# Expert loop of a two-layer MoE trunk: queues held in program order, weights split two pieces ahead

## The chip, the cores and the metric

One core of a Trainium2 chip runs the whole program. Its engines work side by side, each from its own queue: TensorE (matmuls; PE, its weight loads PEld), VectorE (DVE), ScalarE (ACT), GpSimd (POOL) and SyncE (SP, which here only issues loads). The metric is the time of one execution on the device, in microseconds. An instruction waits at the head of its engine's queue until what it needs is there.

## The reference

A trunk of two residual layers on 512 tokens of width 1024, all in fp32. Layer 0 mixes tokens with a state-space and a pooling mixer, layer 1 with stick-breaking attention. Behind each mixer stands the feed-forward part that the change touches:

```
x   = LN(alpha*x + mixer(x))
ple = (p[i] @ Wp) * sigmoid(x @ Wg)
s   = sigmoid(x @ Wr);  best group of 4 experts, then its top 2 of 16 by s + bias;  gates = s normed
h   = silu(x @ w1[e]) * (x @ w3[e])        # 1024 -> 512, for each expert e
ffn = sum_e gates[e] * (h @ w2[e])         # 512 -> 1024
x   = LN(alpha*x + ffn + ple)
```

Each expert has 6 MB of weights (w1, w3, w2), so a layer loads 96 MB of them.

## The kernel before

Each layer's feed-forward part is `ffn`. It sorts the experts by their number of tokens and visits them in a fixed mix, `SEQ`, of ten "big" ones (96 rows of tokens each) and six "small" ones (64 rows). A token's two rows are gathered from DRAM by GpSimd (`gather`), transposed by TensorE into `g` (`load_g`), and an expert's results are scattered back (`scatter`). Rows beyond 96 or 64 go through `overflow`, code in a branch at expert 12 that is skipped when a flag is 0, as here.

A matmul of a big expert is made of three fp32r matmuls (`mm3`): the weights and the tokens are split into a high part (ScalarE's copy to fp32r, L89) and a low part (VectorE's subtraction, L90), and high*high, high*low, low*high are added. A small expert is multiplied in plain fp32 from the raw weights, with w1 and w3 side by side in the array.

Weights come in pieces of 1 MB: four for `up` (w1 and w3, two halves `kh` each) and two for `down`. `plan_ffn` writes the pieces into a list in the order of use: up(e+1, 0), down(e), up(e+1, 1), and so on, with the two pieces of a gate block after expert 7 and of the last one at the end (`GATES`). `prefetch` walks that list and issues loads on SP into "raw" slots (17 of 8 KB a partition, which also hold x, its transposes and `g`). `weights` takes the next piece, splits it on the spot into tiles of two rings (5 high and 6 low tiles; a piece takes two of each) and hands them to the matmuls. `plain` hands out the raw piece of a small expert.

The program is written as: act(e), up(e+1, 0) first piece, turn(e) (transposes of the activation), up(e+1, 0) second piece, down(e), output copies `ysb` (L1147), scatter, load_g(e+2), up(e+1, 1). PSUM has four banks A (up), two B (down and the gate block in the loop), two T (transposes).

The order in which the instructions stand in an engine's queue is not the written one: a scheduler places them, by priority (written order) and by a cost model's idea of when each becomes ready, and it may put a later instruction ahead. The split of a piece is written directly ahead of the matmuls that use it.

Of the kernel before, what the change touches and what calls it, by code (L numbers as in the profile page):

```python
# [2 lines left out]

# [8 lines left out]
AF = mybir.ActivationFunctionType  # L12
# [13 lines left out]
NH = 5  # L26
GATES = (-1, -1, 7, 15)
OVER = 12
SMALL = 64
BIG = 10  # L30
SEQ = (1, 2, 11, 3, 4, 12, 5, 6, 13, 7, 14, 8, 15, 9, 16, 10)
# [10 lines left out]
class Trunk:  # L42
    def __init__(self, ctx, tc, I, out, dbg=None, stop=99):
        self.tc, self.nc, self.I, self.out = tc, tc.nc, I, out
        self.dbgs = dbg or {}
        self.stop = stop
        self.cp = ctx.enter_context(tc.tile_pool(name="cp", bufs=1))
        self.sb = ctx.enter_context(tc.tile_pool(name="sb", bufs=1))
        self.ps = ctx.enter_context(tc.tile_pool(name="ps", bufs=1, space=bass.MemoryType.PSUM))
        self.dp = ctx.enter_context(tc.tile_pool(name="dp", bufs=1, space=bass.MemoryType.DRAM))  # L50
        self.queue = []
        self.loaded = 0
        self.used = 0
        self.raws = {}
        self.cat = None
        self.limit = None
        self.ends = {}
        self.order = {}
        self.eid = {}
# [58 lines left out]
            self.raws[self.loaded] = t  # L118
            self.loaded += 1

    def weights(self, ahead, pool=False):
        i = self.used
        self.prefetch(i + 1 + ahead)
        self.used += 1
        _, k, n, _ = self.queue[i]
        raw = self.raws.pop(i)
        kh = min(k, 1024 // n)
        out = []
        for a in range(0, k, kh):
            h, l = self.ring_pair(f"w{i}_{a}")  # L130
            self.split(h[:, :kh * n], l[:, :kh * n], raw[:, a * n:(a + kh) * n], pool)
            h, l = (t[:, :kh * n].rearrange("p (k n) -> p k n", k=kh) for t in (h, l))
            out += [(h[:, q, :], l[:, q, :]) for q in range(kh)]
        return out

    def consts(self):
        nc, cp = self.nc, self.cp
# [819 lines left out]
    def ffn(self, layer, last):  # L957
# [40 lines left out]
        def gate(c):  # L998
            for _ in gate_parts(c):
                pass  # L1000

        ng = GATES.count(-1)
        pr = self.bank("B", "pB")
# [10 lines left out]
        def rows(e):  # L1014
            return SMALL if SEQ[e] > BIG else CAP

# [19 lines left out]
        def load_g(e):  # L1036
            c = rows(e)
            if c == CAP:
                self.gtile = self.slot(f"g{layer}_{e}", F32R)
                g = self.gtile[:, :2 * KB * c].rearrange("p (a k t) -> p a k t", a=2, k=KB)  # L1040
            else:
                g = self.slot(f"g{layer}_{e}")[:, :KB * c].rearrange("p (k t) -> p k t", k=KB)
            for hf in range(2):
                p = self.bank("T", "pT")[:, :4 * c]
                for k in range(4):
                    nc.tensor.transpose(p[:, k * c:(k + 1) * c], xgs[:c, e % 2, hf * 512 + k:(hf + 1) * 512:4],  # L1046
                                        self.ident[:c, :c])
                ks = slice(hf * 4, hf * 4 + 4)
                p = p.rearrange("p (k t) -> p k t", k=4)
                if c == CAP:  # L1050
                    self.split(g[:, 0, ks], g[:, 1, ks], p)
                elif hf:
                    v.tensor_copy(g[:, ks], p)
                else:
                    nc.scalar.activation(g[:, ks], p, AF.Copy)
            if e + 2 < NE:
                gather(e + 2)
            return e, g

        def banks(e):  # L1060
            return [self.bank("A", "pA") for _ in range(2 if rows(e) == CAP else 1)]

        def up(eg, hh, kh, a):
            e, g = eg
            if rows(e) == CAP:
                w = self.weights(LA)
                for k in range(4):
                    kb = kh * 4 + k
                    self.mm3(hh[a][:CAP], (g[:, 0, kb], g[:, 1, kb]), w[k], kb == 0, kb == KB - 1)
                return  # L1070
            if a == 0:
                self.pair = [self.plain(LA), self.plain(LA)]
            for k in (2 * a, 2 * a + 1):
                kb = kh * 4 + k
                for x in range(2):
                    nc.tensor.matmul(hh[0][x * 64:x * 64 + 64], g[:, kb], self.pair[x][:, k], start=(kb == 0),  # L1076
                                     stop=(kb == KB - 1))

        def act(e, hh):
            t = self.half4("sg")  # L1080
            if rows(e) == CAP:
                sg = t[:CAP, :512]
                nc.scalar.activation(sg, hh[0][:CAP], AF.Silu)
                v.tensor_tensor(sg, sg, hh[1][:CAP], op=OP.mult)  # L1084
                return sg
            nc.scalar.activation(t[64:128, :512], hh[0][0:64], AF.Silu)
            sg = t[0:64, 512:]
            v.tensor_tensor(sg, t[64:128, :512], hh[0][64:128], op=OP.mult)
            return sg
# [16 lines left out]
        def down(e, sT):  # L1106
            hs = [slice(nh * 512, (nh + 1) * 512) for nh in range(2)]
            if rows(e) == CAP:
                py = [self.bank("B", "pB")[:CAP] for _ in hs]
                for a in range(2):  # L1110
                    w = self.weights(LA)
                    for q in range(2):
                        k = 2 * a + q
                        for x, h in enumerate(hs):
                            self.mm3(py[x], (sT[:, 0, k], sT[:, 1, k]), [t[:, h] for t in w[q]], k == 0, k == 3)
            else:
                p = self.bank("B", "pB")
                py = [p[x * 64:x * 64 + 64] for x in range(2)]
                for a in range(2):
                    w = self.plain(LA)  # L1120
                    for q in range(2):
                        k = 2 * a + q
                        for x, h in enumerate(hs):
                            nc.tensor.matmul(py[x], sT[:, k], w[:, q, h], start=(k == 0), stop=(k == 3))  # L1124
            yield from zip(hs, py)

        self.limit = self.ends[layer]
# [3 lines left out]
        for _ in early:  # L1131
            pass
        hh = banks(0)
        up(g, hh, 0, 0)
        up(g, hh, 0, 1)
        gn = load_g(1)
        up(g, hh, 1, 0)
        up(g, hh, 1, 1)
        for e in range(NE - 1):
            sg = act(e, hh)  # L1140
            hh = banks(e + 1)
            up(gn, hh, 0, 0)
            sT = turn(e, sg)
            up(gn, hh, 0, 1)
            ysb = self.half4("ysb")
            for h, py in down(e, sT):
                nc.scalar.activation(ysb[:rows(e), h], py, AF.Copy)  # L1147
            scatter(e, ysb)
            if e == OVER:
                self.overflow(layer, xd, yd)  # L1150
            if e in GATES:
                gate(GATES.index(e))
            g = gn
            if e + 2 < NE:
                gn = load_g(e + 2)
            if e == NE - 3:
                oht = self.last_onehot(self.gtile[:, 2 * KB * CAP:])
                self.ln_setup("ln_ffn", layer)
            up(g, hh, 1, 0)
            up(g, hh, 1, 1)  # L1160
        yts = []
        for i in range(NT):
            yt = self.slot(f"yt{layer}_{i}")
# [161 lines left out]
    def plan_ffn(self, layer):  # L1325
        I = self.I
        wg = I["ple_w_gate"][layer]
        wp = I["ple_w_proj"][layer]

        def gate(c):  # L1330
            self.plan(wg[:, c * 256:(c + 1) * 256], 8, 256)
            self.plan(wp[:, c * 256:(c + 1) * 256], 2, 256)

        def part(e, n, rs, cs=slice(None)):
            r = SEQ[e]
            if r <= 2:
                return I[n][layer, r - 1, rs, cs]

            def dyn():
                x = self.expert(layer, r)  # L1340
                return None if x is None else I[n][layer, bass.ds(x, 1), rs, cs]
            return dyn

        def up(e, kh):
            for n in ("moe_w1", "moe_w3"):
                self.plan(part(e, n, slice(kh * 512, (kh + 1) * 512)), 4, 512, True)

        for c in range(GATES.count(-1)):
            gate(c)
        up(0, 0)  # L1350
        up(0, 1)
        for e in range(NE):
            if e + 1 < NE:
                up(e + 1, 0)
            for nh in range(2):
                self.plan(part(e, "moe_w2", slice(nh * 256, (nh + 1) * 256)), 2, 1024, True)
            if e in GATES:
                gate(GATES.index(e))
            if e + 1 < NE:
                up(e + 1, 1)  # L1360
        self.ends[layer] = len(self.queue)
# [61 lines left out]
```

## Time and profile before

| | |
|---|---|
| three runs | 1269.9, 1266.07, 1269.86 us (median 1269.86) |
| the profiled execution | 1270.47 us, span of its trace 1268.7 us |
| TensorE busy | 1155.3 us, 91% of the span |
| VectorE, ScalarE, GpSimd busy | 790.2, 595.3, 129.7 us |
| mean granted TensorE clock | 0.953 of 2.4 GHz |
| DMA | 285.05 MB, mean 225 GB/s |
| expert loop of layer 0 | about 236 to 552 us of the span |
| expert loop of layer 1 | about 913 to 1225 us of the span |

Matmuls overlap in the pipeline, so the time of a group of them is read from start to start. A row of the waits says which engine and line waited for which, the sum, the number of waits and the longest. The granted clock is a share of 2.4 GHz; at any moment it is 1.0 or 0.5.

### The profile page before, as it was taken

To read this page: it belongs to the slowest core of one execution; us is meant where nothing else is said; L and a number is where in the kernel's file an instruction comes from. 1 tells how busy PE (TensorE), PEld (TensorE's weight loads), DVE (VectorE), ACT (ScalarE), POOL (GpSimd) and SP (SyncE) were. 2 spreads that over 40 slices of the span, in tenths; PEclk is the share of its full clock that TensorE was granted. 3 is DMA by queue.
4 is the path that set the end of the run, shared out by engine and by line. 5 is a ranking of instruction groups with operands and counts; after the bars stand their busy time and mean duration, and the time that the engine had idled before them with its cause. 6 is when DMAs were issued, how large, how long until landed. Compare 5 with 4: busy or idle time off the path is not lost. (4 is left out here: it accounts for less than half of the span.)

```text
span 1268.7 us, 16688 instructions
## 1 busy us (share of the span) xinstructions
PE 1155.3 (91%) x6191; PEld 819.9 (65%) x6191; DVE 790.2 (62%) x1249; ACT 595.3 (47%) x895; POOL 129.7 (10%) x153
## 2 busy tenths in 40 slices
PE   6958989999899887899999999998999899987895
PEld 5847779756467544576867767688865467544564
DVE  7997775765475443477477467756777465453465
ACT  4313531756464443453365456523466455444451
POOL 5010020111010110001000000010111110110001
PEclk9988999999899997799999999998999899988898
DMA  8226651699897996873112014434399997997941
GB/s 254 59 79 210 261 174 65 230 366 395 344 335 287 360 367 234 324 256 100 34 42 92 1 67 159 159 133 142 107 385 373 370 347 267 377 340 279 365 181 66
DMA packets 83663, 285.05 MB, mean 225 GB/s; under 512 B 18816, under 2 KB 42896, under 8 KB 57936
## 3 DMA queue, kind: packets, MB, share of 16 engines
q1 hardware_dynamic: 70032, 256.56, 54.2%
q0 software_dynamic: 8800, 25.19, 6.1%
q10 hardware_dynamic: 4736, 2.10, 0.6%
q8 instruction: 52, 0.85, 0.3%
q14 instruction: 43, 0.35, 0.1%
HBM read 270.45 MB, written 18.61 MB: 228 GB/s over the span
## 5 line engine op out<-in xcount | busy, mean ns | idle before, releaser
L90 DVE TENSOR_TENSOR w_0l<-raw,w_0h 128x1024 fp32r<-128x1024 f32 (+1 forms) x161 | 192.2, 1194 | 59.2 <-ACT w_0h L89 58.4
L89 ACT ACTIVATE w_0h<-raw 128x1024 fp32r<-128x1024 f32 (+1 forms) x161 | 166.4, 1033 | 49.7 <-PE pG L96 27.2
L90 DVE TENSOR_TENSOR w_2l<-raw,w_2h 128x1024 fp32r<-128x1024 f32 x93 | 113.4, 1220 | 47.7 <-ACT w_2h L89 47.6
L89 ACT ACTIVATE w_2h<-raw 128x1024 fp32r<-128x1024 f32 x93 | 97.9, 1053 | 48.2 <-PE pA L96 40.7
L94 PE MATMUL pA<-w_0h,g 128*96 128x512 f32 x160 | 71.5, 447 | 35.4 <-ACT g L89 35.4
L1076 PE MATMUL pA<-raw,g 128*64 128x512 f32 x384 | 97.3, 620 | 0.0
L1147 ACT ACTIVATE ysb<-pB 96x512 f32<-96x512 f32 (+1 forms) x60 | 35.3, 591 | 105.2 <-PE pB L1124 58.8
L1019 POOL DMA_INDIRECT xg<-xd,ixm x32 | 34.4, 1076 | 409.2 <-PE pT L1046 339.2
L95 PE MATMUL pA<-w_0l,g 128*96 128x512 f32 x160 | 67.7, 423 | 3.2 <-DVE w_0l L90 3.2
L96 PE MATMUL pA<-w_0h,g 128*96 128x512 f32 x160 | 68.3, 427 | 2.0 <-DVE g L90 1.9
L94 PEld LDWEIGHTS pA<-w_0h,g 128*96 128x96 f32 x160 | 28.3, 177 | 59.1 <-ACT g L89 44.3
L94 PE MATMUL pA<-w_2h,g 128*96 128x512 f32 x160 | 65.9, 412 | 0.0
L96 PE MATMUL pA<-w_2h,g 128*96 128x512 f32 x160 | 65.3, 408 | 0.0
L95 PE MATMUL pA<-w_2l,g 128*96 128x512 f32 x160 | 65.3, 408 | 0.0
L1026 POOL DMA_INDIRECT yd<-ysb,ixm x30 | 35.3, 1175 | 228.2 <-ACT ysb L1147 180.1
L1076 PEld LDWEIGHTS pA<-raw,g 128*64 128x64 f32 x384 | 25.8, 139 | 43.5 <-issue 39.9
L90 DVE TENSOR_TENSOR w_1l<-raw,w_1h 128x1024 fp32r<-128x1024 f32 x40 | 48.8, 1219 | 3.6 <-ACT w_1h L89 3.2
L696 DVE TENSOR_TENSOR_SCAN kw<-kw 128x128 f32<-128x128 f32 (+3 forms) x64 | 50.3, 813 | 0.9 <-ACT kw L693 0.6
L1046 PEld LDWEIGHTS pT<-ident,xg 96*128 96x128 f32 (+1 forms) x256 | 34.8, 215 | 22.5 <-issue 15.0
L89 ACT ACTIVATE w_1h<-raw 128x1024 fp32r<-128x1024 f32 x40 | 42.0, 1051 | 10.6 <-PE pA L96 10.6
L1046 PE MATMUL pT<-ident,xg 96*128 96x96 f32 (+1 forms) x256 | 37.0, 285 | 10.7 <-PEq L1231 5.0
L1084 DVE TENSOR_TENSOR sg<-sg,pA 96x512 f32<-96x512 f32 x20 | 13.6, 682 | 48.6 <-PE pA L96 48.6
(469 smaller groups left out, 2909.6 us busy)
## 6 DMA issues: line engine op xcount, KB each, us to landing
raw<-in_moe_w_dram SPq DMA_DIRECT2D x192, 1024.0 KB, 8.3
raw<-in_sb_w_qkv_dram SPq DMA_DIRECT2D x12, 1024.0 KB, 6.0
raw<-in_ple_w_gate_dram SPq DMA_DIRECT2D x8, 1024.0 KB, 8.6
yt<-yd SPq DMA_DIRECT2D x8, 1024.0 KB, 7.9
raw<-in_ab_w_out_dram SPq DMA_DIRECT2D x4, 1024.0 KB, 6.5
xd<-x0r POOLq DMA_DIRECT2D x8, 512.0 KB, 4.0
raw<-in_sb_w_out_dram SPq DMA_DIRECT2D x4, 1024.0 KB, 5.8
raw<-in_ab_w_in_dram SPq DMA_DIRECT2D x3, 1024.0 KB, 8.8
```

The costliest lines, as they stand in the source:

```text
L89: return (self.nc.scalar.activation(hi, src, AF.Copy), (self.nc.gpsimd if pool else self.nc.vector).tensor_tensor(lo, src, hi.bitcast(F32) ...
L90: (self.nc.gpsimd if pool else self.nc.vector).tensor_tensor(lo, src, hi.bitcast(F32), op=OP.subtract))
L94: t.matmul(out, s[0], m[0], start=first, stop=False)
L95: t.matmul(out, s[0], m[1], start=False, stop=False)
L96: t.matmul(out, s[1], m[0], start=False, stop=last)
L696: v.tensor_tensor_scan(rv, rv, rv, 1.0, op0=OP.mult, op1=OP.min)
L1019: return nc.gpsimd.indirect_dma_start(out=xgs[:c, e % 2, :], out_offset=None, in_=xd[:, :], in_offset=bass.IndirectOffsetOnAxis(ap=self.ix ...
L1026: nc.gpsimd.indirect_dma_start(out=yd[:, :], out_offset=bass.IndirectOffsetOnAxis(ap=self.iy[:c, r:r + 1], axis=0), in_=src[:c], in_offset ...
L1046: nc.tensor.transpose(p[:, k * c:(k + 1) * c], xgs[:c, e % 2, hf * 512 + k:(hf + 1) * 512:4], self.ident[:c, :c])
L1076: nc.tensor.matmul(hh[0][x * 64:x * 64 + 64], g[:, kb], self.pair[x][:, k], start=(kb == 0), stop=(kb == KB - 1))
L1084: v.tensor_tensor(sg, sg, hh[1][:CAP], op=OP.mult)
L1147: nc.scalar.activation(ysb[:rows(e), h], py, AF.Copy)
```

## The change

Two things. `weights` is cut in two: `cut` splits a piece, `weights` takes a piece that was split earlier if there is one. A new `ahead` splits on from the next piece, skipping pieces of small experts (`whole`), until two split pieces stand ready or four pieces have been looked at; it is called after each piece that TensorE uses in the expert loop and after the gate block. And the body of the loop, now `step` and `rest`, runs under `ordered`, which ties every instruction of TensorE, ScalarE and VectorE to the one written before it on the same engine, so that the scheduler keeps the written order in these three queues. SP and GpSimd are not tied, nor is the code outside the loop.

```diff
+ENGINES = (mybir.EngineType.PE, mybir.EngineType.Activation, mybir.EngineType.DVE)
...
+        self.ready, self.whole, self.chain, self.chained = {}, set(), {}, None
...
-    def weights(self, ahead, pool=False):
-        i = self.used
-        self.prefetch(i + 1 + ahead)
-        self.used += 1
-        _, k, n, _ = self.queue[i]
-        raw = self.raws.pop(i)
+    def cut(self, i):
+        raw, (_, k, n, _) = self.raws.pop(i), self.queue[i]
...
+    def weights(self, ahead):
+        i = self.used
+        self.prefetch(i + 1 + ahead)
+        self.used += 1
+        return self.ready.pop(i) if i in self.ready else self.cut(i)
+
+    def ahead(self, depth):
+        i = self.used
+        self.prefetch(i + depth)
+        while len(self.ready) < 2 and i < min(self.loaded, self.used + 4):
+            if i not in self.ready and i not in self.whole:
+                self.ready[i] = self.cut(i)
+            i += 1
+
+    @contextmanager
+    def ordered(self):
+        block = self.nc.cur_bb
+        traced = block.bb.instructions
+        start = len(traced)
+        yield
+        assert self.nc.cur_bb is block
+        last = self.chain if self.chained is block else {}
+        for i in traced[start:]:
+            if i.engine in ENGINES:
+                if i.engine in last:
+                    self.tc.add_manual_dep(i, last[i.engine], mybir.DependencyInfo(
+                        mybir.DependencyClass.NoSync, mybir.DependencyReason.DATA), reason="order")
+                last[i.engine] = i.name
+        self.chain, self.chained = last, block
...
             for _ in gate_parts(c):
                 pass
+            self.ahead(LA)
...
+                self.ahead(LA)      # in up() and down(), after each piece's matmuls
...
+        def step(e, hh, gn):
+            with self.ordered():
+                sg = act(e, hh)
+                hh = banks(e + 1)
+                up(gn, hh, 0, 0)
+                sT = turn(e, sg)
+                up(gn, hh, 0, 1)
+                ysb = self.half4("ysb")
+                for h, py in down(e, sT):
+                    nc.scalar.activation(ysb[:rows(e), h], py, AF.Copy)
+            scatter(e, ysb)
+            return hh
+
+        def rest(e, hh, g):
+            gn = None
+            with self.ordered():
+                if e in GATES:
+                    gate(GATES.index(e))
+                if e + 2 < NE:
+                    gn = load_g(e + 2)
+                if e == NE - 3:
+                    self.oht = self.last_onehot(self.gtile[:, 2 * KB * CAP:])
+                up(g, hh, 1, 0)
+                up(g, hh, 1, 1)
+            if e == NE - 3:
+                self.ln_setup("ln_ffn", layer)
+            return gn
+
         for e in range(NE - 1):
-            sg = act(e, hh)
...
+            hh = step(e, hh, gn)
             if e == OVER:
                 self.overflow(layer, xd, yd)
-            if e in GATES:
-                gate(GATES.index(e))
...
+            gn = rest(e, hh, gn)
...
+            if r > BIG:
+                self.whole.add(len(self.queue))
```

The two up calls of expert 0 and `load_g(1)` between them, ahead of the loop, are put under `ordered` too.

## Rows read from the trace of the kernel before

**Rows 1.** Page, engines: busy us (share of the span) x instructions.
```profile
PE 1155.3 (91%) x6191; PEld 819.9 (65%) x6191; DVE 790.2 (62%) x1249; ACT 595.3 (47%) x895; POOL 129.7 (10%) x153
```

**Rows 2.** Windows: both loops and stretches; first line names the columns.
```profile
core 0: us, PE busy (x) PEld busy (x) DVE busy (x) ACT busy (x) POOL busy (x), PEclk, DMA share, GB/s
236.00:552.00 316.00, 288.03 (x1300) 175.75 (x1299) 169.60 (x187) 163.30 (x208) 32.91 (x30) 0.94 0.86 326
913.00:1225.00 312.00, 287.74 (x1302) 175.97 (x1301) 170.21 (x187) 163.31 (x209) 33.09 (x30) 0.94 0.88 330
236.00:391.00 155.00, 147.46 (x682) 93.37 (x681) 94.19 (x98) 90.70 (x114) 20.09 (x17) 0.98 0.95 361
...
327.00:340.00 13.00, 7.55 (x22) 3.84 (x17) 6.34 (x7) 7.75 (x10) 0.00 (x0) 0.74 0.93 363
...
495.00:507.00 12.00, 6.49 (x25) 2.83 (x25) 3.37 (x4) 3.31 (x5) 0.00 (x0) 0.72 0.58 205
518.00:538.00 20.00, 15.12 (x59) 11.32 (x56) 6.16 (x8) 8.13 (x11) 0.00 (x0) 0.66 0.85 320
```

**Rows 3.** Waits of TensorE, 236 to 552 us: total us, times, longest us.
```profile
PE pA L94 <- ACT g L89: 17.7, 6, 5.0
PE pT L1046 <- DVEq L1231: 2.9, 1, 2.9
PE pT L1046 <- PEq L1231: 2.7, 1, 2.7
PE pA L95 <- DVE w_0l L90: 1.6, 2, 0.9
```

**Rows 4.** Waits of TensorE, 913 to 1225 us; the other terms as in rows 3.
```profile
PE pT L1046 <- PEq L1231: 2.3, 1, 2.3
```

**Rows 5.** Timeline of TensorE: start us, us, instruction, count, [idle before <- releaser].
```profile
279.80 0.47 PE L94 MATMUL pA<-w_0h,g 128*96 128x512 f32 x1
...
282.76 3.65 PE L1124 MATMUL pB<-raw,sT 128*64 128x512 f32 x16
...
313.17 1.94 PE L1076 MATMUL pA<-raw,g 128*64 128x512 f32 x8
...
332.87 0.74 PE L94 MATMUL pA<-w_0h,g 128*96 128x512 f32 x1 [5.01 <-ACT g L89]
```

**Rows 6.** Timeline of ScalarE around that wait.
```profile
322.68 1.29 ACT L1147 ACTIVATE ysb<-pB 96x512 f32<-96x512 f32 x2 [3.55 <-PE pB L96]
327.94 0.59 ACT L1086 ACTIVATE sg<-pA 64x512 f32<-64x512 f32 x1 [3.96 <-PE pA L1076]
328.55 1.06 ACT L89 ACTIVATE w_0h<-raw 128x1024 fp32r<-128x1024 f32 x1
...
332.35 0.85 ACT L89 ACTIVATE g<-pT 128x384 fp32r<-128x384 f32 x2
```

**Rows 7.** Timeline of SP: issue of two weight loads.
```profile
302.44 0.33 SPq L117 DMA_DIRECT2D raw<-in_moe_w_dram  x1
...
424.82 0.33 SPq L117 DMA_DIRECT2D raw<-in_moe_w_dram  x1
```

**Rows 8.** DMA issues, 236 to 552 us: count, size, median us to landing.
```profile
raw<-in_moe_w_dram SPq DMA_DIRECT2D x86, 1024.0 KB, 8.4
```

**Rows 9.** Groups by form, 236 to 391 us: busy us, mean ns | idle before.
```profile
L89 ACT ACTIVATE w_0h<-raw 128x1024 fp32r<-128x1024 f32 x34 | 35.8, 1053 | 3.6 <-PE pA L96 2.6 <-PE pB L96 1.0
...
L90 DVE TENSOR_TENSOR w_0l<-raw,w_0h 128x1024 fp32r<-128x1024 f32 x34 | 41.4, 1219 | 8.9 <-ACT w_0h L89 8.7
...
L1084 DVE TENSOR_TENSOR sg<-sg,pA 96x512 f32<-96x512 f32 x6 | 4.1, 682 | 13.0 <-PE pA L96 13.0
```

**Rows 10.** Timeline of VectorE: the last expert's one-hot.
```profile
510.65 1.62 DVE L1218 TENSOR_SCALAR ohl<-slotrow,keep,sel 128x128 f32<-128x128 bf16 x6
```

**Rows 11.** Timeline of TensorE: the one-hot's matmuls.
```profile
524.96 3.75 PE L1219 MATMUL pT<-ident,ohl 128*128 128x128 f32 x16 [0.82 <-DVE g L90]
```

**Rows 12.** Waits of SP, 236 to 552 us: total us, times, longest us.
```profile
SPq L117 <- DVE w_2l L90: 91.2, 28, 11.8
```

**Rows 13.** Timeline of ScalarE: the copy of the piece issued at 424.82.
```profile
438.36 1.05 ACT L89 ACTIVATE w_0h<-raw 128x1024 fp32r<-128x1024 f32 x1
```

More of the change, by code (lines that the diff above doesn't have):

```diff
@@ L1 @@
 import math
-from contextlib import ExitStack
+from contextlib import ExitStack, contextmanager
 import concourse.bass as bass
@@ L130, in weights @@
             h, l = self.ring_pair(f"w{i}_{a}")
-            self.split(h[:, :kh * n], l[:, :kh * n], raw[:, a * n:(a + kh) * n], pool)
+            self.split(h[:, :kh * n], l[:, :kh * n], raw[:, a * n:(a + kh) * n])
             h, l = (t[:, :kh * n].rearrange("p (k n) -> p k n", k=kh) for t in (h, l))
@@ L1077, in up @@
                                      stop=(kb == KB - 1))
+            self.ahead(LA)
         def act(e, hh):
@@ L1115, in down @@
                             self.mm3(py[x], (sT[:, 0, k], sT[:, 1, k]), [t[:, h] for t in w[q]], k == 0, k == 3)
+                    self.ahead(LA)
             else:
@@ L1124, in down @@
                             nc.tensor.matmul(py[x], sT[:, k], w[:, q, h], start=(k == 0), stop=(k == 3))
+                    self.ahead(LA)
             yield from zip(hs, py)
@@ L1133, in ffn @@
         hh = banks(0)
[L1134 to L1138, printed above, removed]
-        for e in range(NE - 1):
-            sg = act(e, hh)
[L1141 to L1148, printed above, removed]
+        with self.ordered():
+            up(g, hh, 0, 0)
+            up(g, hh, 0, 1)
+            gn = load_g(1)
+            up(g, hh, 1, 0)
[14 more added lines that the diff above has]
+            gn = None
+            with self.ordered():
+                if e in GATES:
[4 more added lines that the diff above has]
+                    self.oht = self.last_onehot(self.gtile[:, 2 * KB * CAP:])
+                up(g, hh, 1, 0)
+                up(g, hh, 1, 1)
+            if e == NE - 3:
+                self.ln_setup("ln_ffn", layer)
+            return gn
+        for e in range(NE - 1):
+            hh = step(e, hh, gn)
             if e == OVER:
                 self.overflow(layer, xd, yd)
-            if e in GATES:
-                gate(GATES.index(e))
[L1153 to L1160, printed above, removed]
+            gn = rest(e, hh, gn)
+        oht = self.oht
         yts = []
```

## Prediction

> **What bounds the kernel now.** I read the page's engine shares first, then two stretches of the trace, then who waits for whom in them. TensorE is busy 91% of the span [rows 1]; nothing else is near that, so time is won only where TensorE stands still or runs at half clock. The change touches the two expert loops, 236 to 552 us and 913 to 1225 us. There TensorE is busy 288.0 of 316 us and 287.7 of 312 us, so it stands still 28.0 and 24.3 us, and the granted clock has a mean of 0.94 in both [rows 2]. The clock has two levels, 1.2 and 2.4 GHz, so a mean of 0.94 means that 12% of the stretch runs at half rate; 6% of its work time is lost: 0.06 x 316 = 19 us and 0.06 x 312 = 18.7 us. About 47 us of one loop and 43 us of the other are therefore not work. I call that the prize, 90 us in all.
>
> What makes the idle time? In the first loop 17.7 us lie in six waits for one thing, ScalarE's copy of the gathered tokens `g` (L89), before the first matmul of a 96-row ("big") expert; 1.6 us are two waits for VectorE's half of a weight split; 5.6 us are the branch around the overflow code (L1231) [rows 3]. The remaining 3.1 us I leave standing. The second loop repeats 17.7 and 1.6 to the digit and has 2.3 us at the branch [rows 4].
>
> The longest of these waits shows why. TensorE idles 5.01 us before 332.87 [rows 5]. ScalarE copied the last expert's output at 322.68, then did nothing for 3.96 us, because the next entry in its queue was the small expert's `sg`, which needs TensorE's last matmul. Only behind it stood four weight copies (328.55 on) and, behind those, the copy of `g` at 332.35 [rows 6]. So the queue held ready work behind an entry that was not ready. The data had long been there: the first of the two pieces (by its place in the plan) was issued at 302.44 [rows 7], and the median landing is 8.4 us after issue [rows 8], so it lay in SBUF from about 311, 17 us before its copy. It was a question of order, not of supply.
>
> The clock follows: over 327 to 340 us it is 0.74 granted, 13 x 0.26 = 3.4 us lost on top of the 5.01. At the branch (495 to 507) 0.72, 3.4 us; over 518 to 538, where a 4 us wait runs into the one-hot matmuls, 0.66, 6.8 us [rows 2]. Of the first loop's 19 us that leaves 8.8 for the stretches behind the other `g` waits.
>
> **The change, part by part.** (1) After each piece of weights the code now splits on until two pieces stand ready, past the whole (unsplit) pieces of small experts. Read off the program order: while TensorE does the down projection before a small expert's second half, ScalarE and VectorE now split the next big expert's first two pieces, and `g` of the expert after is copied right behind the output copy. Both are what TensorE waited for. So the 17.7 and the 1.6 go: 19.3 us in each loop. (2) Their half-clock stretches go with them: 8.8 us, and half of the 6.8 behind the one-hot (the half that the `g` wait began, 3.4): 12.2 us, taken alike for the second loop, whose mean clock is the same. Gross: 31.5 us a loop, 63 us in all.
>
> Now what comes instead. (3) Does the held order keep pace? A piece of a big expert costs TensorE 2.96 us (279.80 to 282.76, twelve matmuls) [rows 5]; ScalarE two copies of 1.05, 2.1 us, VectorE two subtractions of 1.22, 2.44 us [rows 9]. Over an expert VectorE needs 12 x 1.22 = 14.6 us and some 2.5 for `g`, `sg` and `sT`, 17.1 against TensorE's 6 x 2.96 and 1.9 of transposes, 19.7. It keeps pace with 2.6 us to spare. The ring has 5 high tiles, a piece takes two, so of the piece two ahead the second half can only be written when TensorE is halfway through the piece in use; TensorE then needs it no sooner than 4 us later.
>
> (4) The tight spot is a big expert followed by a small one (six a loop): TensorE covers the activation with 1.94 us only [rows 5]. The last ring pair is released 1.48 us before TensorE ends the expert; copy 1.05, subtraction 1.22, so VectorE is free 0.8 us after that end, does `sg` in 0.68 [rows 9], and the transposes can start at 1.5: 0.4 us to spare. If VectorE is one subtraction late it is 0.8 us short. That bounds it between 0 and 6 x 0.8 = 4.8 us a loop (less than nothing it cannot be, the waits of before being counted already). I take 2, nearer to the row-by-row working than to the late case.
>
> By the Trainium skill's PSUM — Partial Sum matmul accumulation buffer (Engine vs sequencer instructions) ScalarE and VectorE work their queues strictly first in, first out. That speaks against part (1) as much as for it: a split that has to wait, for a landing or for the ring, now holds up every activation behind it. Rows 6 agree, with 3.96 us of that very kind; the sum by it alone is that of the slower rival below.
>
> (5) The gate block inside the loop now follows expert 7's down projection directly, and both PSUM banks it could use hold that projection's output. The first of the two output copies takes half of 1.29 us [rows 6]; with the handoff 0.9 us of waiting. Bounds 0 (another bank order) and 1.3 (both copies).
>
> (6) The last expert's one-hot now stands in the held order, straight behind the copies of `g`, and ahead of a small expert's matmuls. VectorE made six of its eight comparisons in 1.62 us before, beside other TensorE work [rows 10]; now TensorE must wait for 8 x 0.27 = 2.2 us and for the two transpose banks. Its own 16 records took 3.75 us at half clock [rows 11] and are no new work. I take 3 us, between 0 (hidden as before) and 6 (nothing overlaps, clock low).
>
> (7) The overflow branch stays; its 5.6 and 2.3 us and its half clock are in neither sum.
>
> (8) Loads. The plan's order of loads and SP's queue are not touched, but SP's waits are mostly for VectorE's subtractions to free a raw slot (91.2 us in 28 waits for one tile group) [rows 12], so earlier splits issue loads earlier. The loop needs 0.86 x 316 = 272 us of DMA time; in its first half the share was already 0.95 [rows 2]. If the loop shrinks to 292 us, the share must be 0.93. That is near what has been seen, not over it. The tightest piece found: issued 424.82 [rows 7], landing some 8.4 later at 433.2, copied 438.36 [rows 13]: 5 us of margin where the new order wants it about 3 us sooner. I price it at 2 us a loop, between 0 and the rival's 17.
>
> Sum: 63 - 2 x (2 + 0.9 + 3 + 2) = 63 - 16 = 47 us. The profiled execution took 1270.5 us, its span is 1268.7; it is 0.6 above the median of the runs shown, 1269.9. So 1270.5 - 47 - 0.6, about 1223; I write 1222.
>
> **Rivals.** *Loads become the bound.* For it: small experts hold raw slots until TensorE has used them, and in the loop's second half small and big alternate. Against: the 17 us above. If the share reaches only 0.90, a loop lasts 272 / 0.90 = 302 us, 14 us gained each: 1270 - 28 = 1242.
>
> *Nothing new costs.* The one-hot and the gate hide and the steps stay tight: all 63 and up to 12 more from the clock at the one-hot and the branch: 1195 to 1207.
>
> *The held queue stalls TensorE (slower).* At each of the 15 steps of a loop the split two pieces ahead stands in ScalarE's and VectorE's queues before the activation, and waits for the ring or a landing. Place: the transposes of `sg` after the first piece of the next expert. From 63 / 30 = 2.1 us a step on the kernel loses; at 3 us, one copy, one subtraction and `sg` in a row (1.05 + 1.22 + 0.68), it is 90 - 63 = 27 slower: 1297. Against: VectorE's 2.6 us to spare per expert.
>
> *It does not do what it says.* Order and splits stay in effect what they were, since ring or raw slots give no room: 1268 to 1272. Against: when TensorE waited 5 us the ring was empty and the data 17 us old. By the Trainium skill's Perfetto Trace Analysis (Optimization Strategy) gaps that repeat can mean that there is no buffer for the next tile; by that rule a new order would win nothing. These gaps do repeat, but the trace has the cause in the order of ScalarE's queue.
>
> **How the numbers follow.** Forecast, 1207 to 1236: 0.57. Loads: 0.20. Nothing new costs: 0.10. Slower: 0.07. No effect: 0.06. The likeliest is 1222. The range takes the forecast's own, most of the loads' case and half of the cheap one: 1198 to 1250. A measurement of this kernel can tell about 0.3%, 4 us: faster 0.57 + 0.20 + 0.10 = 0.87, same 0.05, slower 0.08.
>
> **What would show it.** Right: in the waits of TensorE in the two loops the `ACT g L89` line falls from 17.7 us to under 3; the loops take 285 to 298 us; DMA share in them 0.90 or more; the half clock is left at the branch and the one-hot. (4) is wrong if waits of the transposes (L1096) for `sg` pass 5 us in a loop; (6) if the one-hot's waits pass 6; (8) if TensorE's or ScalarE's waits name weight loads. The whole is wrong if TensorE's idle time in a loop is over 20 us.

## The result, and the profile after

The changed kernel takes 1228.6 us (median of four: 1223.54, 1224.23, 1232.97, 1233.93) against 1269.6 for the kernel before: a ratio of 0.968 [0.963, 0.974], 41 us faster. A second series gave 1228.1 and 0.969. The forecast was 1222. The four runs lie in two pairs 9 us apart and the profile is of the fastest, 1223.54, so it stands 46.9 us under the profiled run of before where the medians differ by 41.

The page's engine row, to be read beside [rows 1]:

```profile
PE 1132.8 (93%) x6191; PEld 810.6 (66%) x6191; DVE 796.0 (65%) x1249; ACT 599.7 (49%) x895; POOL 125.2 (10%) x153
```

The same instructions ran. The windows, columns as in [rows 2]: both loops, cut where TensorE has run as many instructions as in those rows, then the branch and the one-hot.

```profile
233.00:522.00 289.00, 274.71 (x1300) 170.76 (x1299) 172.88 (x190) 166.91 (x213) 30.73 (x30) 0.98 0.93 359
884.00:1178.00 294.00, 277.92 (x1300) 171.97 (x1299) 174.61 (x190) 167.46 (x213) 30.63 (x30) 0.97 0.91 353
465.00:477.00 12.00, 7.48 (x26) 4.76 (x23) 3.79 (x4) 5.18 (x7) 0.92 (x1) 0.72 0.55 201
488.00:498.00 10.00, 8.09 (x48) 7.35 (x47) 6.46 (x14) 4.30 (x7) 2.25 (x3) 0.83 1.01 410
```

The loops fell from 316 to 289 and from 312 to 294 us. Split each loss as the prediction did. Idle time is now 289 - 274.71 = 14.3 and 16.1 us (28.0 and 24.3 before). The clock costs 0.02 x 289 = 5.8 and 0.03 x 294 = 8.8 us (19 and 18.7 before). So by this reckoning the first loop won 13.7 us of idle time and 13.2 of clock, the second 8.2 and 9.9, and the windows shrank by 27 and 18 us. The means have two digits only, and TensorE's busy time, which fell by 13.3 and 9.8 us, did so not by the clock alone; term (2) below takes the two apart.

TensorE's waits in the first loop, to be read beside [rows 3]: total us, times, longest. PEq and DVEq are the sequencers of TensorE and VectorE, here at the branch (L1277); `ohl` is the last expert's one-hot, a matrix of zeros and ones that VectorE makes by comparisons and TensorE uses.

```profile
PE pT L1127 <- DVE sg L1115: 4.1, 4, 2.0
PE pT L1075 <- PEq L1277: 3.4, 1, 3.4
PE pT L1265 <- DVE ohl L1264: 1.9, 1, 1.9
PE pA L98 <- DVE g L92: 1.5, 1, 1.5
PE pG L96 <- ACT w_0h L91: 1.1, 1, 1.1
PE pT L1075 <- DVEq L1277: 1.1, 1, 1.1
```

The 17.7 us for ScalarE's `g` and the 1.6 for VectorE's half of a split are gone from the list; the activation `sg` stands at its head. In the second loop it is the same, with `sg` and the branch dearer (its 3.2 and the 2.4 behind it):

```profile
PE pT L1127 <- DVE sg L1115: 5.5, 4, 3.6
PE pT L1075 <- PEq L1277: 3.2, 1, 3.2
PE pT L1075 <- issue: 2.4, 1, 2.4
PE pT L1265 <- DVE ohl L1264: 1.8, 1, 1.8
```

Why `g` is no longer late can be seen in ScalarE's timeline around the place of [rows 6]. The copy of `g` (L91) follows the output copies `ysb` at once, ahead of the small expert's `sg`:

```profile
318.46 1.05 ACT L1182 ACTIVATE ysb<-pB 96x512 f32<-96x512 f32 x2
319.41 0.86 ACT L91 ACTIVATE g<-pT 128x384 fp32r<-128x384 f32 x2
322.31 0.59 ACT L1117 ACTIVATE sg<-pA 64x512 f32<-64x512 f32 x1 [2.04 <-PE pA L1106]
```

ScalarE's waits have a line that neither loop had before, first loop and second:

```profile
ACT w_0h L91 <- DMA raw<-in_moe_w_dram: 32.5, 20, 3.8
...
ACT w_0h L91 <- DMA raw<-in_moe_w_dram: 24.6, 15, 3.4
```

57 us of waiting for weights that have not landed. TensorE has only some 30 us of idle time in both loops together, so most of this wait does not reach it. At a few places it does. The timeline of all engines at the dearest one, in the second loop:

```profile
1090.37 1.06 ACT L91 ACTIVATE w_0h<-raw 128x1024 fp32r<-128x1024 f32 x1 [1.82 <-DMA raw<-in_moe_w_dram]
1091.33 1.04 ACT L91 ACTIVATE w_1h<-raw 128x1024 fp32r<-128x1024 f32 x1
...
1092.28 0.57 ACT L1114 ACTIVATE sg<-pA 96x512 f32<-96x512 f32 x1
1092.60 1.22 DVE L92 TENSOR_TENSOR w_1l<-raw,w_1h 128x1024 fp32r<-128x1024 f32 x1
1093.74 0.68 DVE L1115 TENSOR_TENSOR sg<-sg,pA 96x512 f32<-96x512 f32 x1
...
1094.47 0.92 PE L1127 MATMUL pT<-ident,sg 96*128 96x96 f32 x4 [3.60 <-DVE sg L1115]
...
1095.32 3.68 PE L1106 MATMUL pA<-raw,g 128*64 128x512 f32 x8
```

A split that is needed only later waits 1.82 us for its load; behind it stand `sg` on ScalarE and the second subtraction on VectorE, and TensorE idles 3.60 us. It then runs at half clock: the last row takes 3.68 us, 1.94 at full clock [rows 5]. By the Trainium skill's PSUM — Partial Sum Buffer (Engine vs sequencer instructions) ScalarE and VectorE take their queues strictly in turn; these rows agree.

### The profile page after: what moved, and what is told of

It reads as the page before. It is cut to its first block, busy times and chain, and to the rows that moved or that the text cites. A ratio compares the mean times of both kernels' runs of the same rounds, so it can differ in the third digit from the quotient of the medians.

```text
span 1221.9 us, 16728 instructions
## 1 busy us (share of the span) xinstructions
PE 1132.8 (93%) x6191; PEld 810.6 (66%) x6191; DVE 796.0 (65%) x1249; ACT 599.7 (49%) x895; POOL 125.2 (10%) x153
## 5 line engine op out<-in xcount | busy, mean ns | idle before, releaser
L91 ACT ACTIVATE w_0h<-raw 128x1024 fp32r<-128x1024 f32 (+1 forms) x161 | 166.9, 1037 | 95.8 <-DMA raw<-in_moe_w_dram 57.1
L92 DVE TENSOR_TENSOR w_2l<-raw,w_2h 128x1024 fp32r<-128x1024 f32 x93 | 113.5, 1221 | 20.1 <-ACT w_2h L91 20.1
L91 ACT ACTIVATE w_2h<-raw 128x1024 fp32r<-128x1024 f32 x93 | 98.1, 1055 | 38.7 <-PE pA L98 25.2
L1106 PE MATMUL pA<-raw,g 128*64 128x512 f32 x384 | 92.1, 611 | 0.0
L96 PE MATMUL pA<-w_0h,g 128*96 128x512 f32 x160 | 67.7, 423 | 0.0
L98 PE MATMUL pA<-w_0h,g 128*96 128x512 f32 x160 | 64.3, 402 | 3.0 <-DVE g L92 3.0
L96 PE MATMUL pA<-w_2h,g 128*96 128x512 f32 x160 | 64.2, 401 | 0.0
L97 PE MATMUL pA<-w_0l,g 128*96 128x512 f32 x160 | 63.8, 399 | 0.0
L98 PE MATMUL pA<-w_2h,g 128*96 128x512 f32 x160 | 63.5, 397 | 0.0
L92 DVE TENSOR_TENSOR w_1l<-raw,w_1h 128x1024 fp32r<-128x1024 f32 x40 | 48.8, 1221 | 7.7 <-ACT w_1h L91 7.7
L1106 PEld LDWEIGHTS pA<-raw,g 128*64 128x64 f32 x384 | 24.6, 138 | 41.8 <-issue 35.9
L91 ACT ACTIVATE w_1h<-raw 128x1024 fp32r<-128x1024 f32 x40 | 42.2, 1055 | 11.4 <-PE pA L98 11.2
L1055 POOL DMA_INDIRECT yd<-ysb,ixm x30 | 30.1, 1003 | 150.8 <-ACT ysb L1182 118.3
L1156 PE MATMUL pB<-raw,sT 128*64 128x512 f32 x192 | 43.8, 598 | 0.5 <-DVE sT L1134 0.5
L92 DVE TENSOR_TENSOR w_4l<-raw,w_4h 128x1024 fp32r<-128x1024 f32 x20 | 24.4, 1221 | 29.3 <-ACT w_4h L91 29.2
## 6 DMA issues: line engine op xcount, KB each, us to landing
raw<-in_moe_w_dram SPq DMA_DIRECT2D x192, 1024.0 KB, 11.1
```

Of the source, the lines that this page charges most:

```text
L91: return (self.nc.scalar.activation(hi, src, AF.Copy), (self.nc.gpsimd if pool else self.nc.vector).tensor_tensor(lo, src, hi.bitcast(F32) ...
L92: (self.nc.gpsimd if pool else self.nc.vector).tensor_tensor(lo, src, hi.bitcast(F32), op=OP.subtract))
L96: t.matmul(out, s[0], m[0], start=first, stop=False)
L97: t.matmul(out, s[0], m[1], start=False, stop=False)
L98: t.matmul(out, s[1], m[0], start=False, stop=last)
L1055: nc.gpsimd.indirect_dma_start(out=yd[:, :], out_offset=bass.IndirectOffsetOnAxis(ap=self.iy[:c, r:r + 1], axis=0), in_=src[:c], in_offset ...
```

## The experiments

All are edits of the changed kernel, in three series, each timed beside the kernel before (1266.6 to 1267.8 us). The changed kernel itself is in the last series alone, so the others are best compared by the ratio: it is to the kernel before, with its 95% interval.

| kernel | median us | ratio |
|---|---|---|
| order not held | 1262.4 | 0.995 [0.993, 0.997] |
| order held on TensorE alone | 1251.8 | 0.989 [0.985, 0.992] |
| on ScalarE and VectorE | 1217.0 | 0.960 [0.958, 0.963] |
| on ScalarE alone | 1212.7 | 0.956 [0.954, 0.958] |
| one piece ahead | 1221.0 | 0.963 [0.958, 0.967] |
| half loads | 1211.2 | 0.955 [0.951, 0.959] |
| activation ahead of the split | 1226.7 | 0.966 [0.962, 0.970] |
| no overflow code | 1217.7 | 0.960 [0.956, 0.963] |
| one ahead, gate and one-hot moved | 1207.3 | 0.953 [0.950, 0.956] |
| two ahead, both moved | 1217.2 | 0.960 [0.958, 0.962] |
| one ahead, both moved, ScalarE and VectorE held | 1223.7 | 0.966 [0.963, 0.968] |
| the changed kernel again | 1228.1 | 0.969 [0.965, 0.972] |

### Which part does it: the order or the earlier splits?

**Order not held.** The splits stand two pieces ahead in the program, but the scheduler places them.

```diff
-            if i.engine in ENGINES:
+            if False and i.engine in ENGINES:
```

> Splits two pieces ahead, but no order held: the scheduler may again place later entries first. Theory (TensorE waited for splits and copies of g that stood too late in ScalarE's queue; written earlier they get a higher priority and come earlier, but nothing keeps the copy of g and sg in place): some two thirds of the gain, 1235 to 1250 us, TensorE's waits for ACT g L91 between 3 and 15 us in both loops together. Rival 1 (the splits ahead are all of it): 1222 to 1234 us, waits as in the changed kernel. Rival 2 (the held order is all of it): 1258 to 1272 us, the waits for ACT g back at over 25 us in both loops together.

TensorE's waits in its first loop begin with the old one:

```profile
PE pA L96 <- ACT g L91: 16.6, 6, 5.0
```

The second loop has the same 16.6. The gain is 5 us of 41 and the wait is what it was (17.7). Writing the splits earlier, without an order that keeps them there, wins next to nothing. My theory, which gave both a share, fell; rival 2 came true in the time and in the waits.

**One piece ahead.**

```diff
-        while len(self.ready) < 2 and i < min(self.loaded, self.used + 4):
+        while len(self.ready) < 1 and i < min(self.loaded, self.used + 4):
```

> Order held, but one piece split ahead in place of two. Theory (depth two is needed, because the activation, the copies of the output and of g stand between two splits in the same queue): TensorE waits 1 to 2 us at each of 30 steps for w_0l or w_2l, 1250 to 1280 us. Rival (one piece is enough, and the loads are wanted one piece, 3 us, later, so ScalarE's waits for weight loads shrink from 57 us to under 30): 1212 to 1228 us.

It is 7 us under the changed kernel (the intervals overlap); TensorE waits 0.8 us a loop for a split. So the depth of two is not needed, and my theory fell here too. The rival's time held, but not its reason: ScalarE's waits for loads did not shrink (30.5 and 39.0 us, against 32.5 and 24.6).

**Order held on two engines, on TensorE alone, on ScalarE alone.**

```diff
-ENGINES = (mybir.EngineType.PE, mybir.EngineType.Activation, mybir.EngineType.DVE)
+ENGINES = (mybir.EngineType.Activation, mybir.EngineType.DVE)   # first
+ENGINES = (mybir.EngineType.PE,)                                # second
+ENGINES = (mybir.EngineType.Activation,)                        # third
```

> As the changed kernel, with the order held for ScalarE and VectorE alone; TensorE's queue is the scheduler's again. Theory (the gain is the order of ScalarE's and VectorE's queues: the copy of g and the splits no longer stand behind an activation that is not ready): 1221 to 1236 us, TensorE's waits for ACT g under 3 us a loop. Rival (TensorE's order matters as much, since a matmul placed early waits there for its split): 1240 to 1262 us.

> As the changed kernel, with the order held for TensorE alone. Theory (as before: ScalarE's and VectorE's queues are what counts): 1250 to 1268 us, the six waits for ACT g back with some 16 us a loop, as in the run with splits ahead and no order. Rival (TensorE's order carries the gain, the others follow it): 1221 to 1240 us.

> As the changed kernel, with the order held for ScalarE alone. Theory (the ready work stood behind an unready entry in ScalarE's queue; VectorE mostly follows ScalarE's copies): 1214 to 1228 us, as with both held. Rival (VectorE's own order puts subtractions of later pieces ahead of the low part of g and of sg): 1230 to 1255 us, with waits for DVE g over 5 us a loop.

With TensorE alone held, the waits of the first loop are:

```profile
PE pA L96 <- ACT g L91: 6.9, 5, 3.1
PE pA L98 <- DVE g L92: 6.3, 5, 1.6
PE pT L1265 <- DVE g L92: 3.6, 1, 3.6
```

`g` is still late, by 13 us for the two halves and 3.6 more at the one-hot. In the time my theory held; its 16 us for ScalarE's half came out at 6.9. With ScalarE alone held, the first loop has:

```profile
PE pA L1106 <- DMA raw<-in_moe_w_dram: 3.4, 1, 3.4
PE pA L98 <- DVE g L92: 1.1, 1, 1.1
PE pT L1127 <- DVE sg L1115: 0.8, 1, 0.8
PE pT L1075 <- PEq L1277: 0.6, 1, 0.6
PE pB L96 <- ACT sT L91: 0.6, 1, 0.6
PE pA L96 <- ACT g L91: 0.4, 1, 0.4
```

That is 0.4 us of waiting for ScalarE's half of `g`, and the one-hot, the branch and the late `sg` have all shrunk. That an unordered TensorE and VectorE put other work there is likely, but was not followed. With the splits two pieces ahead, as in the run without any order, the order of ScalarE's queue gives the whole gain, and more than all three orders together. TensorE's order alone gives 15 us, so the shares do not add up; VectorE's alone was not tried. In its cause my theory held in the first and the third run, but both came out under its range: all four runs of the first lie below 1221 us, and the third's median is 1.3 us below 1214.

### What does the held order cost?

**Half loads.** Small experts load half of each piece and use it twice, 18 MB less a loop; their results are not the reference's.

```diff
+            if self.loaded in self.whole:
+                self.nc.sync.dma_start(dst[:, :k // 2], src[:, :k // 2])
...
-  self.pair[x][:, k]       # small up;   small down: w[:, q, h]
+  self.pair[x][:, k % 2]   #                         w[:, 0, h]
```

> Small experts load half of each weight piece and use that half twice, so that their result is another; every matmul, split and copy stays, and a loop loads 18 MB less of 88. Theory (what is left in the loops beside the branch and the one-hot is late loads: ScalarE waits 57 us for them, and sg stands behind): ScalarE's waits for weight loads fall under 10 us, TensorE's waits for sg (9.6 us in both loops) under 3 us with a half-clock stretch of 6.8 us gone in the second loop: 1208 to 1220 us. Rival (the waits for loads are hidden, what is left is order): 1224 to 1234 us, the waits for sg stay over 7 us.

ScalarE's waits for loads, first and second loop (all weights' lines):

```profile
ACT w_0h L91 <- DMA raw<-in_moe_w_dram: 5.4, 2, 3.8
...
ACT w_0h L91 <- DMA raw<-in_moe_w_dram: 1.2, 1, 1.2
```

57 us became 6.6, the wait for `sg` fell to 0.8 us in each loop, and the time by 17 (11 between the profiled runs). So late loads are worth some 17 us over both loops in the changed kernel. 8 us of that are TensorE's own waits for `sg`; where the rest comes from was not followed. My theory held.

**Activation ahead of the split.** After the last piece of an expert the splits ahead are written behind `act`, not in front of it.

```diff
-            up(g, hh, 1, 1)
+            up(g, hh, 1, 1, False)     # expert 0: no ahead() behind this piece
...
             sg = act(e, hh)
+            self.ahead(LA)
...
-                up(g, hh, 1, 1)
+                up(g, hh, 1, 1, e == NE - 2)
```

> The activation (silu and its product) of an expert is written ahead of the split that follows its last up matmuls. Theory (sg waits because it stands behind a split that waits for a load): TensorE's waits for sg L1115 fall from 9.6 us to under 3 us in both loops together, the half-clock stretch behind the 3.6 us wait goes: 1214 to 1224 us; ScalarE still waits for loads. Rival (the late load then holds TensorE at the next piece instead): waits for w_0l or w_0h take their place, 1224 to 1234 us.

The wait for `sg` fell to 0.3 us in each loop, but the second loop now has, for the transposed activation `sT`,

```profile
PE pB L1158 <- DVE sT L1136: 5.6, 2, 3.4
```

and the first one 3.3 us of it: 8.9 in both, where `sg` had 9.6. In the written order the split now stands in front of `sT`, one step on. The time is that of the changed kernel. The rival held, with the wait at `sT` and not, as it said, at the next weights: the wait had only moved.

**No overflow code.** The branch, whose flag is 0 here, is left out.

```diff
-            if e == OVER:
-                self.overflow(layer, xd, yd)
```

> The changed kernel without the overflow code and its branch (never taken with these inputs). Theory (the branch costs TensorE its 4.5 and 5.6 us of waiting and half of 6.8 us of half clock in each loop, and nothing else takes its place): 17 us less than the changed kernel, 1207 to 1215 us. Rival (the loads catch up while TensorE stands at the branch; without it they are late instead): 1217 to 1229 us, ScalarE's waits for weight loads grow by 5 us or more in a loop.

1217.7 us, 11 less than the changed kernel: short of theory's 1207 to 1215, just inside the rival's range. The rival's reason is not borne out, though: ScalarE's waits for loads are 31.2 and 27.5 us, not 5 longer in either loop. In the first loop the branch's waits are gone, and those of `sg` and the one-hot are dearer than in the changed kernel:

```profile
PE pT L1127 <- DVE sg L1115: 5.1, 4, 1.9
PE pT L1263 <- DVE ohl L1262: 3.2, 1, 3.2
```

In both loops together 10.1 us of waits at the branch went and 2.2 came there, and the mean clock did not rise (0.970 over the profiled run, 0.971 in the changed kernel): the half clock that theory took off stayed.

### A better version

**One ahead, gate and one-hot moved.** The depth is one, as above; the transposes and copies of the next `g` are written ahead of the gate block, the last expert's one-hot behind the small expert's matmuls.

```diff
-                if e in GATES:
-                    gate(GATES.index(e))
                 if e + 2 < NE:
                     gn = load_g(e + 2)
-                if e == NE - 3:
-                    self.oht = self.last_onehot(self.gtile[:, 2 * KB * CAP:])
+                if e in GATES:
+                    gate(GATES.index(e))
                 up(g, hh, 1, 0)
                 up(g, hh, 1, 1)
+                if e == NE - 3:
+                    self.oht = self.last_onehot(self.gtile[:, 2 * KB * CAP:])
```

> One piece ahead in place of two, the last expert's one-hot written behind the small expert's second half (so that VectorE makes it while TensorE multiplies), and the gather's transposes ahead of the gate block (so that they cover the output copies). Theory (each of these waits is its own and not cover for late loads): the one-hot's 1.9 and 1.8 us and its 3.4 us half-clock stretches go, 6 to 8 us against the run with one piece ahead: 1211 to 1217 us. Rival (loads are late by as much as TensorE gains): 1218 to 1226 us.

It beats both kernels, and theory: 1207.3 us. Its loops by windows, columns as above:

```profile
234.00:517.00 283.00, 273.75 (x1303) 169.04 (x1302) 171.22 (x189) 164.39 (x215) 31.16 (x30) 0.99 0.95 367
878.00:1161.00 283.00, 273.95 (x1302) 168.81 (x1301) 170.84 (x189) 164.35 (x215) 31.16 (x30) 0.99 0.95 366
```

Idle time is 9.3 and 9.1 us, at a clock of 0.99. The waits for the one-hot and for VectorE's half of `g` are gone from both loops. ScalarE still waits 30.9 us for loads in its first loop, nearly as long as in the changed kernel (32.5), so the length of that wait does not set the time. That what stands behind it does is my reading.

**Two ahead, both moved** (the same edit, the depth left at two).

> The moves of the one-hot and of the gather's transposes with two pieces ahead kept and the order held for all three engines. Theory (the moves are worth 6 to 10 us by themselves, one piece ahead the rest, since a split two pieces ahead asks for its load 3 us sooner and holds up sg when it is late): 1213 to 1222 us. Rival (the depth is nothing, the moves are all): 1203 to 1211 us, as with one piece ahead.

1217.2 us: the two moves together are worth 11 us at a depth of two (they were not tried one by one), and going back to one another 10. Theory held.

**The moved version with ScalarE and VectorE held, TensorE not** (both edits from above).

> The two edits that won put together: one piece ahead with the one-hot and the gather's transposes moved, and the order held for ScalarE and VectorE alone. Theory (TensorE left free fills the branch's and the one-hot's waits by itself, the moves take the same waits away, so the gains overlap): 1200 to 1208 us, TensorE's waits at the branch under 3 us a loop. Rival (they add up, 10 and 14 us below the changed kernel's 1222 to 1228): 1192 to 1200 us. Second rival (free of order, TensorE takes matmuls early whose weights are late): 1208 to 1216 us.

1223.7 us, worse than with either edit alone (1207.3 and 1217.0): no theory gave that. TensorE's waits are as short as in the moved version: 8.5 and 6.4 us idle in its windows, against 9.3 and 9.1. But TensorE is busy for longer. The page's group of the small experts' up matmuls, in the moved version and then here:

```profile
L1106 PE MATMUL pA<-raw,g 128*64 128x512 f32 x384 | 90.3, 602 | 0.0
```

```profile
L1106 PE MATMUL pA<-raw,g 128*64 128x512 f32 x384 | 109.3, 614 | 2.6 <-ACT g L1084 2.6
```

19 us more for the same 384 matmuls. TensorE's timeline shows how:

```profile
357.81 1.07 PE L1106 MATMUL pA<-raw,g 128*64 128x512 f32 x2
...
361.54 1.94 PE L1106 MATMUL pA<-raw,g 128*64 128x512 f32 x8
363.41 0.72 PE L1127 MATMUL pT<-ident,sg 96*128 96x96 f32 x4
364.06 1.93 PE L1106 MATMUL pA<-raw,g 128*64 128x512 f32 x6
```

Normally the two matmuls of a pair, w1 and w3 side by side in the array, start 7 ns apart, and the next pair 0.43 us later: eight in 1.94 us. Here the scheduler moved single ones: two take 1.07 us, and six as long as eight, since two of them run alone. By the start times in the trace 56 of the 576 small-expert matmuls run alone here, none in the moved version and in the changed kernel. At 0.43 us for each two that is 12 of the 16 us between the two versions. (The 19 us of the group also count where a lone matmul overlaps those of other lines.)

Lone matmuls are not new. Wherever TensorE is not held some are alone: 16 in the kernel before, 24 with no order, 40 with ScalarE and VectorE held and 40 with ScalarE alone. Two of those in the kernel before:

```profile
391.41 1.07 PE L1076 MATMUL pA<-raw,g 128*64 128x512 f32 x2
```

So the order on TensorE won the changed kernel eight slots of 0.43 us, 3.4 us, by pairs alone. And 40 lone ones, 8.6 us, did not keep the version with ScalarE and VectorE held from beating the changed kernel by 11: a free TensorE brought the idle time there down from 14.3 and 16.1 us to 9.1 and 9.5, and the clock up from 0.98 and 0.97 to 1.00 and 0.98. In the moved version that idle time was mostly gone already, and the lost pairs weigh more.

**The changed kernel again** (no edit).

> The changed kernel once more, beside these runs: 1222 to 1234 us, ratio to the kernel before 0.963 to 0.974. If it comes out at 1215 to 1220, what the runs with one piece ahead or with TensorE free seem to win is the difference of chips.

0.969, as in the first series.

## Why the prediction was right

It was right in its cause, a queue in the wrong order, and near in its sum: 46.9 us off the profiled execution, where 47 were forecast, but 41 between the medians. That the profiled pair agrees to 0.1 us is luck. The loops won 27 and 18 us where 23.6 each were forecast, 45 in all, and the other 2 lie outside them; and terms that were too large and too small cancel.

- **(1), the waits for `g` and splits, 19.3 us a loop:** gone in both loops, as forecast. But the step laid this to splits that run two pieces ahead, together with the order. The runs put it on the order of ScalarE's queue: both with splits two ahead, the ratio is 0.956 with that order and 0.995 with none. The earlier splits alone do not do it. Whether the order needs them is open, since an order held with no split ahead was not tried.
- **(2), half clock, 12.2 us a loop:** 13.2 and 9.9 by the prediction's own reckoning, which counts half clock also where TensorE stands still, on top of the idle time. Counted only where TensorE is busy, the clock records of the two traces give 16.2 us lost before and 5.1 after in the first loop, 15.2 and 8.5 in the second: 11.1 and 6.7 won, below the forecast. The rest of the fall in busy time (13.3 and 9.8) is not clock; 1.7 us a loop of it are the pairs that TensorE's order keeps together, for which the prediction has no term. The half clock that is left lies, in the main, at the branch (0.72), the one-hot (0.83) and behind the late `sg`.
- **(4), `sg` before a small expert, 2 us a loop:** mis-sized; 4.1 and 5.5, the second over the 5 us that were to count as wrong. The step asked whether VectorE is one subtraction late. The trace shows the split in front of `sg` waiting for its load.
- **(8), loads, 2 us a loop:** mis-sized. ScalarE's waits do name weight loads, which was the mark of a wrong step. The two steps belong together: taking the late loads away takes 8 us of `sg` waits away and is worth 17 us over both loops, where (4) and (8) had 8. The margin of 5 us [rows 13] was read at one piece of a slower loop. The rival "loads become the bound" had the resource, but not the mechanism: the share did not stop at 0.90 (0.93 and 0.91; 0.95 in the moved version).
- **(5), the gate, 0.9 us:** no wait of that kind in the loop. Instead 1.5 us for VectorE's half of `g`, which is absent at one piece ahead and where `g` is written ahead of the gate.
- **(6), the one-hot, 3 us:** 1.9 and 1.8 us of waiting, within the forecast's bounds. VectorE's comparisons took 2.14 us in one go (2.2 forecast). The half clock over them, 0.17 x 10 = 1.7 us, comes to it in the first loop.
- **(7), the branch, in neither sum:** 4.5 us in the first loop (5.6 before), 5.6 in the second (2.3 before). That is 1.1 us more and 3.3 less won, half of the 9 us by which the loops differ.
- **The slower rival, 2.1 us a step lost:** its mechanism is what the rows at 1090.37 show, but at four steps of a loop and for 4.1 to 5.5 us, not at fifteen for 31.5. Of the 5.5 us one wait is 3.6.

By the Trainium skill's Perfetto Trace Analysis (Optimization Strategy) a gap that repeats can mean too few buffers. It does not hold here: with the same buffers and the same splits ahead, the repeated `g` wait went from 16.6 us to 0.4 by the order of ScalarE's queue alone.

What stays open: why the branch's waits differ between the two loops; why the loads are late by less with ScalarE and VectorE held and TensorE free (17.4 and 8.7 us of ScalarE's waits in the two loops, against 32.5 and 24.6); and 4 of the 16 us that lie between the two moved versions, which are in TensorE's busy time too, since its waits are no longer.

## What to carry to other kernels

When the busiest engine waits for data that landed long ago, look in the queue of the engine that hands it over for an entry that is not ready, and hold the written order on that queue first; here, with the splits written ahead, one queue gave all of it. Once it is held, look at what stands behind a wait at its head, and not at the wait's length: work that is not urgent (splits ahead, a one-hot, a gate) belongs behind the copies that the busiest engine needs next. A held order on the busiest engine itself cut both ways here: it kept pairs of matmuls together, and it cost time where idle stretches were left that other work could fill.

## What the hardware showed that was not expected

In these traces two 64-column matmuls run at once in the array where they follow each other directly in TensorE's queue, and only there. One that other matmuls part from its partner costs a whole slot of 0.43 us, and the busy time of the same 384 matmuls went from 90.3 to 109.3 us when TensorE's order was let go. The waits and the idle time do not show it: they did not grow. The group's busy time and the start times do.
